# Order of split-precision matmuls within a converted piece of weights: by form instead of by triple

## The chip, the cores and the metric

The kernel runs on one core of a Trainium2 chip. A core has a matrix engine (TensorE, PE in the profile, with its weight loads shown as PEld), VectorE (DVE), ScalarE (ACT), GpSimd (POOL) and SyncE (SP), which issues most DMAs. The metric is the device time of one execution in microseconds; lower is better. Before the change it is 2777.81 us, the median of 3 runs (2772.61 to 2782.02).

## The reference

One decoder residual block over 512 positions with model width 2048, in float32:

```
h = rms_norm(x, norm1_g)
z = h @ w_in                                   # 2048 -> r, k, v, three LoRA inputs, q, k, v, two gates
o_rw  = rwkv7_mix(token_shift(z_rw), ...)      # 16 heads of 64, a recurrence over the positions
o_att = swa_attention(q, k, v, ...)            # 16 query heads, 4 key heads, window 128, sinks
x = x + (sigmoid(z_g1) * (o_rw @ w_b1) + sigmoid(z_g2) * (o_att @ w_b2)) @ w_out
u = rms_norm(x, norm2_g) @ w_up                # 2048 -> 2 x 5632
c = causal convolution of u, width 3
x = x + (silu(c_gate) * c_val) @ w_down        # 5632 -> 2048
```

## The kernel before

Every large matrix product is computed from split operands. A float32 operand `a` becomes a high part `whi` (or `xhi`, `hhi`; type float32r, 32 bits wide, written by ScalarE) and a low part `wlo` (`xlo`, `hlo`; bfloat16, written by VectorE as the difference). `top(x)` reads the upper 16 bits of each element of a high part as bfloat16, so with a stride of two. One product of two 128-deep tiles is then three matmuls that add into the same PSUM bank: high x high (32-bit), top x low (16-bit), low x top (16-bit). They are called a triple here. A 32-bit matmul is one instruction of the program that brings its own weight load; a 16-bit one is a separate LDWEIGHTS and a MATMUL. In the profile both loads are PEld rows.

A "piece" is what one conversion covers, one `whi` and one `wlo` tile. Three places use pieces:

- `project` (L273), the input projection and the two branch projections. A piece is four 128 x 128 weight tiles (`load_w`, 256 KB); the moving operand is 512 positions wide. 352 pieces: 72 output tiles of four pieces, then 32 of two. The matmuls go into the list `stream`. While the input projection runs, attention and the RWKV-7 recurrence run beside it: their small PE steps (L531 to L875) are placed between matmuls of the stream, some of them tied by `behind` to a counted place in `stream`. A scheduler orders the rest of this stage on every engine by its own costs.
- `steps_of` (L1042), the output projection ("o") and the down projection ("dn"). Both are done as seven products of half size (Strassen's way, `PRODUCTS`), added in the two groups of PSUM banks X and Y. A piece is 128 x 1024 weights as the moving operand, in two halves `e` of 512; the stationary operand is two tiles `t` of `hhi`, `hlo`. So a piece has four triples, one for each PSUM bank. There are 210 pieces. At the end of each product `taken_out` (L1064) adds the four banks into the result on VectorE; behind the last product the result is stored.
- `Block.mm` (L1182), the up projection, also in seven products of half size ("P1" to "Q4") for each of 44 column blocks. A piece has eight weight tiles of 128 x 128; the moving operand is 256 positions wide. 308 pieces of eight triples. The order on each engine is the program's (`pin`): `prep(i + 2)` converts the piece after next, `mm(i)` multiplies, `out(i)` takes the PSUM bank away.

Converted tiles lie in rings: four deep for `project` (`wp["hl"]`), three deep for the other two (`hlp`). A `whi` tile is free again when the last matmul that reads it, or its upper halves, is done.

Of the kernel before, what the change touches and what calls it, by code (L numbers as in the profile page):

```python
# [19 lines left out]
P = 128  # L20
S = 512
NT = S // P
# [113 lines left out]
def block_kernel(ctx: ExitStack, tc: tile.TileContext, d: Dims, a: dict, out: bass.AP):  # L136
    nc = tc.nc
    act, dve, pool, pe, sync = nc.scalar, nc.vector, nc.gpsimd, nc.tensor, nc.sync
# [54 lines left out]
    def rsqrt_small(pl, ss, scale, eps, mx=None, tag="rq"):  # L193
        n = ss.shape[-1]
        tl = [pl.tile([P, 8], F32, name=f"{tag}{i}", tag=f"{tag}{i}", bufs=2)[:, :n] for i in range(3)]
        v, y, t = tl
        if mx is not None:
            dve.tensor_scalar(v, ss, mx, None, op0=ALU.max)
        else:
            dve.tensor_scalar(v, ss, scale, eps, op0=ALU.mult, op1=ALU.add)  # L200
        dve.tensor_scalar(t.bitcast(I32), v.bitcast(I32), 1, None, op0=ALU.logical_shift_right)
        dve.tensor_scalar(y.bitcast(I32), t.bitcast(I32), -1, 0x5F3759DF, op0=ALU.mult, op1=ALU.add)
        dve.tensor_scalar(v, v, -0.5, None, op0=ALU.mult)
        for _ in range(3):
            dve.tensor_tensor(t, y, y, op=ALU.mult)
            dve.tensor_tensor(t, t, v, op=ALU.mult)
            dve.scalar_tensor_tensor(y, t, 1.5, y, op0=ALU.add, op1=ALU.mult)
        return y

    pin = tc.keep_in_program_order  # L210
# [9 lines left out]
    def quarter(w, src, c):  # L220
        return sum_d[w][src][c] if isinstance(src, str) else a["w_" + w][src[0], src[1], 2 * c : 2 * c + 2]

    jobs, up_jobs = [], []
    for f in range(NPRE):
        w, t = a["w_up"][f], {n: up_d[f, n] for n in ("s3", "s1", "P6", "P3")}
# [19 lines left out]
    stream = []  # L245

    def top(x):
        x = x.bitcast(BF16)
        return x[(slice(None),) * (len(x.shape) - 1) + (slice(1, None, 2),)]
# [5 lines left out]
    def load_w(src):  # L255
        nk, ncol = src.shape[1:]
        n = nk * ncol
        raw = wp["raw"].tile([P, 512], F32, name="raw", tag="raw")[:, :n].rearrange("p (k c) -> p k c", c=ncol)
        wp["last"] = sync.dma_start(raw, src)
        hi = wp["hl"].tile([P, 512], F32R, name="whi", tag="whi")[:, :n].rearrange("p (k c) -> p k c", c=ncol)  # L260
        lo = wp["hl"].tile([P, 512], BF16, name="wlo", tag="wlo")[:, :n].rearrange("p (k c) -> p k c", c=ncol)
        act.activation(hi, raw, AF.Copy)  # L262
        dve.tensor_tensor(lo, raw, hi.bitcast(F32), op=ALU.subtract)  # L263
        wp["n"] += 1
        if wp["n"] in wp["after"]:
            wp["after"].pop(wp["n"])()
        elif wp["step"] == 3 and wp["n"] <= HELD:
            pass
        elif wp["n"] % wp["step"] == 0 or wp["n"] in extra:
            sums_along()()  # L270
        return hi, lo

    def project(acc, src, xhi, xlo, pre=()):  # L273
        nk = src.shape[1]
        for k0 in range(0, nk, 4):
            n = min(4, nk - k0)
            whi, wlo = pre[k0 // 4] if k0 // 4 < len(pre) else load_w(src[:, k0 : k0 + n])
            for j in range(n):
                k = k0 + j
                first, last = k == 0, k == nk - 1  # L280
                stream.append(pe.matmul(acc, whi[:, j], xhi[:, k], start=first, stop=False))  # L281
                stream.append(pe.matmul(acc, top(whi[:, j]), xlo[:, k], start=False, stop=False))  # L282
                stream.append(pe.matmul(acc, wlo[:, j], top(xhi[:, k]), start=False, stop=last))  # L283


    id16 = cstp.tile([P, P], F16, name="id16")
    def big(pl, nm, tag, dt=F32R):
        return pl.tile([P, BIG], dt, name=nm, tag=tag)

    def by_k(t, n=NK):  # L290
        return t[:, : n * S].rearrange("p (k s) -> p k s", s=S)
# [3 lines left out]
    if True:  # L295
        xhi = by_k(big(big1, "xhi", "h1"))
        xlo = by_k(big(big1, "xlo", "l1", BF16))
# [5 lines left out]
        first = {d.c_ka: []}  # L303
# [29 lines left out]
        def ztile(c0):  # L333
            acc = accp.tile([P, S], F32, name="acc", tag="acc")
            project(acc, zt[c0], xhi, xlo, first.pop(c0, ()))
            return acc
# [5 lines left out]
        r = rsqrt_small(p0, ssum, 1.0 / d.D, RMS_EPS)  # L342
        spread = []
        with tc.tile_pool(name="x0_ps", bufs=1, space=PSUM) as ps0:
            ps = ps0.tile([P, S], F32, name="ps_r")
# [53 lines left out]
        with ExitStack() as pt:  # L399
# [4 lines left out]
            def small():  # L404
                return mps.tile([P, S], F32, name="mi", tag="mi")
# [53 lines left out]
            for t in range(1, NKV):  # L459
                for c0, then in ((d.c_ka, keys), (d.c_va, values)):  # L460
                    acc = ztile(c0 + t * P)
# [25 lines left out]
            for g in range(NHK):  # L487
# [7 lines left out]
                for n in range(NT):  # L495
                    ts = slice(n * P, (n + 1) * P)
                    k0 = 0 if n else BLK
                    nk = 2 * BLK - k0
# [13 lines left out]
                    mx, es, den, rc = (st[:, i] for i in range(4))  # L512
# [15 lines left out]
                    for kb in kbs:  # L528
                        ps = small().rearrange("p (h c) -> p h c", c=P)
# [3 lines left out]
                    ps = small()  # L533
                    for kb in kbs:
                        for i in range(2):
                            pe.matmul(ps, vhl[:, n - 1 + kb, g].rearrange("p e c -> p (e c)"),  # L536
                                      phl[i][:, kb].rearrange("p h c -> p (h c)"),
                                      start=kb == kbs[0] and i == 0, stop=kb == kbs[-1] and i == 1)
                    ol = ap_.tile([HD, S], F32, name="ol", tag="ol", bufs=2)
                    act.activation(ol, ps[HD:P], AF.Copy)  # L540
                    ps, ol = (x[0:HD].rearrange("p (e j c) -> p e j c", e=2, c=P) for x in (ps, ol))
# [5 lines left out]
        with ExitStack() as pr:  # L547
# [18 lines left out]
            def wtile(tag, bufs=1):  # L566
                return wk.tile([P, S], F32, name=tag, tag=tag, bufs=bufs)
# [10 lines left out]
            acc = ztile(d.c_wd)  # L578
# [5 lines left out]
            acc = ztile(d.c_ad)  # L584
# [3 lines left out]
            for i in range(NG):  # L588
                acc = ztile(d.c_gd + i * P)
                t = wtile("lw")  # L590
# [353 lines left out]
    KH = NK // 2  # L944
    TH = S // 2
    NQW = DH // S
# [25 lines left out]
    with ExitStack() as pbb:  # L972
# [8 lines left out]
        for m, i in order:  # L981
            hi, lo, r0, n, gi = parts[i]
# [9 lines left out]
            acc = accp.tile([P, S], F32, name="acc", tag="acc")  # L992
            project(acc, a["w_b"][m].rearrange("p (k c) -> p k c", c=P)[:, r0 : r0 + n], hi, lo)
            if second:
                w = min(XC, d.D)
                for e in range(m * XC, (m + 1) * XC, w):
                    t, c0 = divmod(e, d.D)
# [31 lines left out]
    def raw_tile(nm="raw", n=6):  # L1029
        return rwp.tile([P, WC], F32, name=nm, tag=nm, bufs=n)  # L1030
# [11 lines left out]
    def steps_of(w, i, acc, c, pl, got=None):  # L1042

        _, start, src, _, _ = PRODUCTS[i]
        make, hhi, hlo = got or fetch(w, i, c, pl)
        if not got:
            make()
        for q in range(2):
            wr = raw_tile()
            sync.dma_start(wr, quarter(w, src, c)[q])  # L1050
            whi, wlo = (hlp.tile([P, WC], t, name=f"w{e}", tag=f"w{e}") for e, t in (("hi", F32R), ("lo", BF16)))
            act.activation(whi, wr, AF.Copy)  # L1052
            dve.tensor_tensor(wlo, wr, whi.bitcast(F32), op=ALU.subtract)  # L1053
            fst, lst = start and c + q == 0, c == NB[w] - 1 and q == 1
            for t in range(NT // 2):
                ts = slice(t * P, (t + 1) * P)
                for e in range(NQW):
                    dst, es = acc[t][e], slice(e * S, (e + 1) * S)
                    for j, (l, r) in enumerate((
                            (hhi[:, q, ts], whi[:, es]), (hlo[:, q, ts], top(whi[:, es])), (top(hhi[:, q, ts]), wlo[:, es]))):  # L1060
                        pe.matmul(dst, l, r, start=fst and j == 0, stop=lst and j == 2,  # L1061
                                  skip_group_check=True)

    def taken_out(i, acc, xr, scale, done):  # L1064
        ci, tj, sign = PRODUCTS[i][4]
# [86 lines left out]
    class Block:  # L1152
# [29 lines left out]
        def mm(self, n):  # L1182
            if n == "P1":
                x = ups.tile([P, S], F32, name="X", tag="X")
                self.X = x[:, :TH]
                self.Z = x[:, TH:] if self.f < NPRE else upy.tile([P, S], F32, name="Z", tag="Y")[:, :TH]
            if n == "P7":
                self.Y = upy.tile([P, S], F32, name="Y", tag="Y")[:, :TH]
            into = {"P2": "Z", "P7": "Y", "Q4": "Y"}.get(n, "X")
            ps = getattr(self, "Z" if self.apart and n in ("P5", "P3") else into)  # L1190
            start = n in ("P1", "P7") or n == "P2" and self.f >= NPRE or n == "P5" and self.apart
            whi, wlo = (x.rearrange("p (k c) -> p k c", c=P) for x in self.hl.pop(n))
            xh, xl = bq[{"P1": "b11", "P2": "b21", "P7": "t3", "P6": "t2", "P5": "t1", "Q4": "t4", "P3": "b22"}[n]]
            for k in range(KH):
                last = k == KH - 1
                for i, (l, r) in enumerate(((whi[:, k], xh[:, k]), (top(whi[:, k]), xl[:, k]), (wlo[:, k], top(xh[:, k])))):
                    pin(pe.matmul(ps, l, r, start=start and k + i == 0, stop=last and i == 2,  # L1197
                                  skip_group_check=True))

        def out(self, n):  # L1200
            if n == "P7":
# [140 lines left out]
    with tc.tile_pool(name="sqp", bufs=1, side="right", reuse_waits="tile") as sqp:  # L1342
        yx = ExitStack()
        py = yx.enter_context(tc.tile_pool(name="psY", bufs=1, space=PSUM, side="right", reuse_waits="tile"))
        acc = {"X": banks(px, "X"), "Y": banks(py, "Y")}
        for i in range(len(PRODUCTS)):
            nm = PRODUCTS[i][0]
            last = i == len(PRODUCTS) - 1
# [113 lines left out]
    with ExitStack() as pd:  # L1462
        pxy = pd.enter_context(tc.tile_pool(name="psD", bufs=1, space=PSUM, reuse_waits="tile"))
        acc = {n: banks(pxy, n) for n in "YX"}
# [94 lines left out]
```

## Time and profile before

| | |
|---|---|
| median of 3 runs | 2777.81 us (2772.61 to 2782.02) |
| profiled execution, its time | 2778.65 us |
| its span | 2776.9 us |
| PE busy | 2730.4 us (98%) |
| DVE busy | 2000.0 us (72%) |
| ACT busy | 1341.0 us (48%) |
| DMA moved | 623.80 MB, mean 225 GB/s |
| input projection, attention and RWKV | about 10 to 1130 us of the span |
| branch projections | about 1130 to 1305 us |
| output projection | about 1305 to 1460 us |
| up projection | about 1460 to 2348 us |
| down projection | about 2348 to 2772 us |

The profile is of one execution. A row of the timeline gives start (us from the span's start), duration (us), engine, line, operation, output and inputs with shapes, and how many instructions it stands for; in brackets the idle time of the engine before it and what ended it. A row of weight loads is PEld; the time between the starts of two neighbours says how fast the array takes them, since the duration of one record reaches beyond the start of the next. A row of the waits gives who waited for what: us in total, how often, and the longest. A row of busy time in a stretch gives the stretch, its length, then PE, PEld, DVE, ACT and POOL busy with their counts, the granted clock, the share of the DMA engines and GB/s.

### The profile page before, as it was taken

How to read it: one execution, taken by the hardware profiler on the slowest of the kernel's cores; microseconds unless marked ns; L12 is line 12 of the kernel's file. 1: busy time of each engine (PE TensorE's matmuls, PEld its weight loads, DVE VectorE, ACT ScalarE, POOL GpSimd, SP SyncE). 2: the span in 40 equal slices, each digit the busy share in tenths (PEclk: the TensorE clock that was granted, in tenths of full speed). 3: DMA queues.
4: the chain of work that ended last, by engine and by line, in shares of the span. 5: the costliest groups of instructions: out<-in, count | busy, mean ns of one | idle time of the engine just before them, and what ended most of it. 6: DMA issues, size and time to landing. Idle time of an engine off the chain costs nothing.

```text
span 2776.9 us, 45675 instructions
## 1 busy us (share of the span) xinstructions
PE 2730.4 (98%) x17227; PEld 1705.7 (61%) x17410; DVE 2000.0 (72%) x3476; ACT 1341.0 (48%) x2245; POOL 232.0 (8%) x308
## 2 busy tenths in 40 slices
PE   8999999999999999999999999999999999999999
PEld 3454555555555555444448788888888887444444
DVE  6787777787787774545678788787878788555555
ACT  5455435544544553322465555545554545444443
POOL 0001111111111001011000011111110110000000
PEclk9999999999999999999999999999999999999999
DMA  6557788778878767788775888988898888877775
GB/s 230 151 157 206 202 208 214 207 188 234 219 200 214 178 175 231 241 247 274 246 255 187 235 230 230 246 240 233 225 245 242 226 233 259 303 241 239 253 255 184
DMA packets 228333, 623.80 MB, mean 225 GB/s; under 512 B 24960, under 2 KB 45072, under 8 KB 227088
## 3 DMA queue, kind: packets, MB, share of 16 engines
q1 hardware_dynamic: 159552, 445.23, 49.0%
q0 software_dynamic: 37216, 136.33, 25.4%
q10 hardware_dynamic: 31344, 39.31, 4.1%
q8 instruction: 136, 2.23, 0.3%
q14 instruction: 85, 0.70, 0.1%
HBM read 571.16 MB, written 191.18 MB: 275 GB/s over the span
## 4 chain that ended last, share of the span: by engine, by line
PE 83%; DVE 8%; DMA 3%; issue 3%; ACT 2%; SPq 0%; POOL 0%; ACTq 0%; DVEq 0%; POOLq 0%
PE X L1197 17%; PE X L1061 10%; PE acc L281 9%; PE acc L283 9%; PE Y L1061 9%; PE Y L1197 8%; PE acc L282 8%; PE Z L1197 4%; DVE wlo L263 1%; PE psG L820 1%; PE psS L829 1%; DMA rsb<-rsd 1%; PE bulk L757 1%; PE bulk L805 1%; PE mi L536 1%
## 5 line engine op out<-in xcount | busy, mean ns | idle before, releaser
L281 PE MATMUL acc<-xhi,whi 128*128 128x512 f32 x1152 | 666.4, 578 | 10.5 <-ACT whi L262 10.4
L283 PE MATMUL acc<-xhi,wlo 128*128 128x512 bf16 x1108 | 432.5, 390 | 6.3 <-DVE wlo L263 1.4
L282 PE MATMUL acc<-xlo,whi 128*128 128x512 bf16 x1079 | 423.0, 392 | 0.0
L1053 DVE TENSOR_TENSOR wlo<-raw,whi 128x1024 bf16<-128x1024 f32 x210 | 256.9, 1225 | 203.9 <-ACT whi L1052 202.4
L262 ACT ACTIVATE whi<-raw 128x512 fp32r<-128x512 f32 x352 | 220.3, 627 | 336.4 <-PE acc L282 249.5
L1052 ACT ACTIVATE whi<-raw 128x1024 fp32r<-128x1024 f32 x210 | 221.8, 1057 | 287.6 <-PE X L1061 116.5
L282 PEld LDWEIGHTS <-whi 128*128 128x128 bf16 x1408 | 141.6, 101 | 329.7 <-issue 321.0
L263 DVE TENSOR_TENSOR wlo<-raw,whi 128x512 bf16<-128x512 f32 x352 | 239.7, 688 | 127.9 <-ACT whi L262 116.2
L281 PEld LDWEIGHTS acc<-xhi,whi 128*128 128x128 f32 x1152 | 220.1, 191 | 123.5 <-ACT whi L262 12.8
L1197 PEld LDWEIGHTS <-whi 128*128 128x128 bf16 x2464 | 239.0, 97 | 90.6
L1180 DVE TENSOR_TENSOR wlo<-raw,whi 128x1024 bf16<-128x1024 f32 x184 | 224.9, 1223 | 75.3 <-ACT whi L1178 74.1
L1061 PE MATMUL X<-whi,hhi 128*128 128x512 f32 x480 | 276.9, 577 | 0.1
L1197 PE MATMUL X<-b,whi 128*128 128x256 f32 x1472 | 272.2, 323 | 0.2 <-ACT whi L1178 0.2
L1197 PE MATMUL X<-t,whi 128*128 128x256 f32 (+1 forms) x1408 | 260.3, 323 | 1.5 <-ACT u L1225 1.5
L1197 PE MATMUL Y<-t,whi 128*128 128x256 f32 (+1 forms) x1408 | 260.4, 323 | 0.0
L1197 PEld LDWEIGHTS <-wlo 128*128 128x128 bf16 x2464 | 246.4, 100 | 4.7 <-DVE wlo L1180 4.7
L1178 ACT ACTIVATE whi<-a 128x1024 fp32r<-128x1024 f32 x124 | 130.7, 1054 | 203.5 <-DVE a L1173 199.9
L1061 PEld LDWEIGHTS <-hlo 128*128 128x128 bf16 x840 | 80.6, 96 | 212.2 <-issue 212.2
L1061 PE MATMUL Y<-whi,hhi 128*128 128x512 f32 x360 | 207.8, 577 | 0.0
L1197 PE MATMUL X<-b,wlo 128*128 128x256 bf16 x736 | 204.3, 278 | 1.1 <-DVE wlo L1180 1.1
L1178 ACT ACTIVATE whi<-raw 128x1024 fp32r<-128x1024 f32 x184 | 192.5, 1047 | 20.8 <-ACT whi L1178 13.0
L1180 DVE TENSOR_TENSOR wlo<-a,whi 128x1024 bf16<-128x1024 f32 x124 | 151.9, 1225 | 66.9 <-ACT whi L1178 66.2
(387 smaller groups left out, 5398.0 us busy)
## 6 DMA issues: line engine op xcount, KB each, us to landing
raw<-in_w_up_dram SPq DMA_DIRECT2D x170, 512.0 KB
raw<-in_w_z_dram SPq DMA_DIRECT2D x288, 256.0 KB
s_dn<-in_w_dn_dram POOLq DMA_DIRECT2D x88, 512.0 KB, 7.4
raw<-s_dn SPq DMA_DIRECT2D x88, 512.0 KB
raw<-in_w_up_dram POOLq DMA_DIRECT2D x80, 512.0 KB, 8.5
raw<-in_w_dn_dram SPq DMA_DIRECT2D x66, 512.0 KB
s_dn<-in_w_dn_dram SPq DMA_DIRECT2D x44, 512.0 KB
s_dn<-s_dn SPq DMA_DIRECT2D x44, 512.0 KB
```

The source lines that it names most:

```text
L262: act.activation(hi, raw, AF.Copy)
L263: dve.tensor_tensor(lo, raw, hi.bitcast(F32), op=ALU.subtract)
L281: stream.append(pe.matmul(acc, whi[:, j], xhi[:, k], start=first, stop=False))
L282: stream.append(pe.matmul(acc, top(whi[:, j]), xlo[:, k], start=False, stop=False))
L283: stream.append(pe.matmul(acc, wlo[:, j], top(xhi[:, k]), start=False, stop=last))
L536: pe.matmul(ps, vhl[:, n - 1 + kb, g].rearrange("p e c -> p (e c)"), phl[i][:, kb].rearrange("p h c -> p (h c)"), start=kb == kbs[0] and i ...
L1052: act.activation(whi, wr, AF.Copy)
L1053: dve.tensor_tensor(wlo, wr, whi.bitcast(F32), op=ALU.subtract)
L1061: pe.matmul(dst, l, r, start=fst and j == 0, stop=lst and j == 2, skip_group_check=True)
L1178: pin(act.activation(hi, t, AF.Copy))
L1180: return lambda: pin(dve.tensor_tensor(lo, t, hi.bitcast(F32), op=ALU.subtract))
L1197: pin(pe.matmul(ps, l, r, start=start and k + i == 0, stop=last and i == 2, skip_group_check=True))
```

## The change

In all three places the order of the matmuls of one piece is changed, and nothing else. Before, the triples follow each other. Now all high x high matmuls of the piece come first, then all top x low, then all low x top. The flags that open and close an accumulation move with the first and the last matmul of a bank. The number of matmuls and loads, the operands, the conversions and the transfers are the same.

```diff
 project:
-            for j in range(n):
-                k = k0 + j
-                first, last = k == 0, k == nk - 1
-                stream.append(pe.matmul(acc, whi[:, j], xhi[:, k], start=first, stop=False))
-                stream.append(pe.matmul(acc, top(whi[:, j]), xlo[:, k], start=False, stop=False))
-                stream.append(pe.matmul(acc, wlo[:, j], top(xhi[:, k]), start=False, stop=last))
+            ops = [[(whi[:, j], xhi[:, k0 + j]) for j in range(n)],
+                   [(top(whi[:, j]), xlo[:, k0 + j]) for j in range(n)],
+                   [(wlo[:, j], top(xhi[:, k0 + j])) for j in range(n)]]
+            for i, part in enumerate(ops):
+                for j, (l, r) in enumerate(part):
+                    stream.append(pe.matmul(acc, l, r, start=k0 + i + j == 0, stop=k0 + n == nk and i == 2 and j == n - 1))
 steps_of:
-            for t in range(NT // 2):
-                ts = slice(t * P, (t + 1) * P)
-                for e in range(NQW):
-                    dst, es = acc[t][e], slice(e * S, (e + 1) * S)
-                    for j, (l, r) in enumerate((
-                            (hhi[:, q, ts], whi[:, es]), (hlo[:, q, ts], top(whi[:, es])), (top(hhi[:, q, ts]), wlo[:, es]))):
-                        pe.matmul(dst, l, r, start=fst and j == 0, stop=lst and j == 2,
-                                  skip_group_check=True)
+            for j in range(3):
+                for t in range(NT // 2):
+                    ts = slice(t * P, (t + 1) * P)
+                    for e in range(NQW):
+                        dst, es = acc[t][e], slice(e * S, (e + 1) * S)
+                        l, r = ((hhi[:, q, ts], whi[:, es]), (hlo[:, q, ts], top(whi[:, es])), (top(hhi[:, q, ts]), wlo[:, es]))[j]
+                        pe.matmul(dst, l, r, start=fst and j == 0, stop=lst and j == 2, skip_group_check=True)
 Block.mm:
-            for k in range(KH):
-                last = k == KH - 1
-                for i, (l, r) in enumerate(((whi[:, k], xh[:, k]), (top(whi[:, k]), xl[:, k]), (wlo[:, k], top(xh[:, k])))):
-                    pin(pe.matmul(ps, l, r, start=start and k + i == 0, stop=last and i == 2,
-                                  skip_group_check=True))
+            for i in range(3):
+                for k in range(KH):
+                    l, r = ((whi[:, k], xh[:, k]), (top(whi[:, k]), xl[:, k]), (wlo[:, k], top(xh[:, k])))[i]
+                    pin(pe.matmul(ps, l, r, start=start and k + i == 0, stop=k == KH - 1 and i == 2, skip_group_check=True))
```

Three places on PE, in the order of the built program. A row is line, operation, output<-inputs and the output's size; a MATMUL without an LDWEIGHTS ahead of it is a 32-bit one.

First a product of the up projection (Y is the PSUM bank, t the factor on the right in its two parts). Before:

```order
L1197 MATMUL Y<-t_15027,whi 128x256
L1197 LDWEIGHTS whi
L1197 MATMUL Y<-t_15028,whi 128x256
L1197 LDWEIGHTS wlo
L1197 MATMUL Y<-t_15027,wlo 128x256
```

Now (the pairs of LDWEIGHTS and MATMUL are each there eight times; the start is shown):

```order
L1196 MATMUL Z<-b_13632,wlo 128x256
L1196 MATMUL Y<-t_15027,whi 128x256 x8
L1196 LDWEIGHTS whi
L1196 MATMUL Y<-t_15028,whi 128x256
L1196 LDWEIGHTS whi
```

Eight 32-bit matmuls now stand in a row, and one change from 32 to 16 bits is left where there were eight.

Second a step of the recurrence beside the input projection: psU (L823) and psS (L829) are steps of the RWKV chain, between them lie copies on ScalarE and VectorE; acc is a bank of the projection. Before:

```order
L281 MATMUL acc<-xhi,whi 128x512
L823 MATMUL psU<-GY,BX 128x128
L282 LDWEIGHTS whi
L282 MATMUL acc<-xlo,whi 128x512
L283 LDWEIGHTS wlo
L283 MATMUL acc<-xhi,wlo 128x512
L281 MATMUL acc<-xhi,whi 128x512
L282 LDWEIGHTS whi
L282 MATMUL acc<-xlo,whi 128x512
L283 LDWEIGHTS wlo
L283 MATMUL acc<-xhi,wlo 128x512
L829 MATMUL psS<-UV,W_2861 128x64 x2
```

Now:

```order
L823 MATMUL psU<-GY,BX 128x128
L283 LDWEIGHTS wlo
L283 MATMUL acc<-xhi,wlo 128x512
L283 MATMUL acc<-xhi,whi 128x512 x2
L829 MATMUL psS<-UV,W_2861 128x64 x2
L283 MATMUL acc<-xhi,whi 128x512 x2
```

The steps of the chain still stand between matmuls of the projection and cut some pieces; here three of these stand between psU and psS where there were five. All steps from psU to psS together have 230 where there were 240.

Third the last piece of the down projection (X with four numbers are its four PSUM banks). Before:

```order
L1061 MATMUL X_25473<-whi,hhi 128x512
L1061 LDWEIGHTS hlo
L1061 MATMUL X_25473<-whi,hlo 128x512
L1061 LDWEIGHTS hhi
L1061 MATMUL X_25473<-wlo,hhi 128x512
L1061 MATMUL X_25474<-whi,hhi 128x512
L1061 LDWEIGHTS hlo
L1061 MATMUL X_25474<-whi,hlo 128x512
L1061 LDWEIGHTS hhi
L1061 MATMUL X_25474<-wlo,hhi 128x512
```

Now:

```order
L1061 LDWEIGHTS hhi
L1061 MATMUL X_25471<-wlo,hhi 128x512 [waits DVE_49]
L1061 LDWEIGHTS hhi
L1061 MATMUL X_25472<-wlo,hhi 128x512
L1061 LDWEIGHTS hhi
L1061 MATMUL X_25473<-wlo,hhi 128x512
L1061 LDWEIGHTS hhi
L1061 MATMUL X_25474<-wlo,hhi 128x512
```

The last matmuls of the four banks, which `taken_out` waits for, now follow each other directly at the very end.

## The prediction

> **What bounds the kernel now.** I read the page's totals and its chain first, then PE's waits, then single matmuls in the timeline.
>
> ```profile
> span 2776.9 us, 45675 instructions
> PE 2730.4 (98%) x17227; PEld 1705.7 (61%) x17410; DVE 2000.0 (72%) x3476; ACT 1341.0 (48%) x2245; POOL 232.0 (8%) x308
> PE 83%; DVE 8%; DMA 3%; issue 3%; ACT 2%; SPq 0%; POOL 0%; ACTq 0%; DVEq 0%; POOLq 0%
> PE X L1197 17%; PE X L1061 10%; PE acc L281 9%; PE acc L283 9%; PE Y L1061 9%; PE Y L1197 8%; PE acc L282 8%; PE Z L1197 4%; DVE wlo L263 1%; PE psG L820 1%; PE psS L829 1%; DMA rsb<-rsd 1%; PE bulk L757 1%; PE bulk L805 1%; PE mi L536 1%
> ```
>
> TensorE sets the time: 83% of the chain that ended last, and nearly all of that on the three places that the diff touches (L281 to L283, L1061, L1197). A busy PE is not PE at its peak, because a matmul's record is longer than the step to the next. So I work with steps between starts. First the up projection (L1197, 256 columns); the first row is from the chain of waits, the next four are weight loads, the last two matmuls.
>
> ```profile
> 2308.56 2.83 PE X L1197 x24
> ...
> 2000.18 0.19 PEld L1197 LDWEIGHTS Z<-b,whi 128*128 128x128 f32 x1
> 2000.41 0.10 PEld L1197 LDWEIGHTS <-whi 128*128 128x128 bf16 x1
> 2000.42 0.10 PEld L1197 LDWEIGHTS <-wlo 128*128 128x128 bf16 x1
> 2000.53 0.19 PEld L1197 LDWEIGHTS Z<-b,whi 128*128 128x128 f32 x1
> ...
> 2000.18 0.28 PE L1197 MATMUL X<-t,wlo 128*128 128x256 bf16 x1
> 2000.53 0.28 PE L1197 MATMUL Z<-b,wlo 128*128 128x256 bf16 x1
> ```
>
> 24 matmuls take 2.83 us: 0.3538 a triple. The 32-bit load starts with the wlo matmul before it (2000.18), so it is fetched ahead, under that matmul. The 16-bit load of whi starts only 0.23 later, when wlo and the 32-bit matmul are both through: 0.115 each. It is not fetched ahead of a 32-bit matmul. From there to the next wlo matmul are 0.12 (2000.41 to 2000.53), in which lie the load of whi and its matmul. The second 16-bit load follows 0.01 to 0.02 behind the first: that much a 16-bit load holds up what comes behind it. The same at 512 columns, L1061 and L281:
>
> ```profile
> 1400.39 0.19 PEld L1061 LDWEIGHTS X<-whi,hhi 128*128 128x128 f32 x1
> 1400.83 0.10 PEld L1061 LDWEIGHTS <-hlo 128*128 128x128 bf16 x1 [0.25 <-issue]
> 1401.08 0.19 PEld L1061 LDWEIGHTS X<-whi,hhi 128*128 128x128 f32 x1
> ...
> 1007.07 0.19 PEld L281 LDWEIGHTS acc<-xhi,whi 128*128 128x128 f32 x1
> 1007.53 0.10 PEld L282 LDWEIGHTS <-whi 128*128 128x128 bf16 x1 [0.27 <-issue]
> 1007.54 0.10 PEld L283 LDWEIGHTS <-wlo 128*128 128x128 bf16 x1
> 1007.76 0.19 PEld L281 LDWEIGHTS acc<-xhi,whi 128*128 128x128 f32 x1
> ```
>
> Triples of 0.69, split 0.44 and 0.25 (L1061), 0.46 and 0.23 (L281). Each triple has one change from a 32-bit to a 16-bit matmul, and at each the 16-bit load stands open.
>
> **The change, part by part.** No matmul, load, conversion or transfer is added or taken away. What goes are changes of form: in the built order 2464 become 308 in the up products, 839 become 210 at L1061, 1257 become 331 in the projections (pieces are split by other PE work there). 3711 go.
>
> What takes their place are 32-bit matmuls behind 32-bit ones, and 16-bit ones behind 16-bit ones with their loads fetched ahead. The trace has the first at 512 columns, six in a row at L875; and loads of both forms in rows of eight with 128 columns (L740 32-bit, L805 16-bit).
>
> ```profile
> 410.50 0.40 PE L875 MATMUL bulk<-gdlo,wghi 128*128 128x512 f32 x1
> ...
> 411.66 0.40 PE L281 MATMUL acc<-xhi,whi 128*128 128x512 f32 x1
> 410.51 0.19 PEld L875 LDWEIGHTS bulk<-gdhi,wglo 128*128 128x128 f32 x1
> 410.74 0.19 PEld L875 LDWEIGHTS bulk<-gdhi,wghi 128*128 128x128 f32 x1
> 1000.24 1.04 PE L740 MATMUL bulk<-ident,BKK 128*128 128x128 f32 x8
> 1000.13 0.90 PEld L740 LDWEIGHTS bulk<-ident,BKK 128*128 128x128 f32 x8
> 335.14 0.62 PE L805 MATMUL bulk<-id,XIW 128*128 128x128 f16 x8 [0.38 <-DVE XIW L801]
> ...
> L740 PE MATMUL bulk<-ident,BKK x64: 272/272/273, 323.4 to 1001.0; 128*128 128x128 f32 x64
> L805 PE MATMUL bulk<-id,XIW x256: 217/219/230, 335.1 to 1035.0; 128*128 128x128 f16 x128
> ```
>
> Five steps from 410.50 to 411.66 are 0.232 each, and each load starts with the matmul before it: 32-bit behind 32-bit is fetched ahead. Its step is what 32-bit costs in a triple (0.44 to 0.46 for two), within 0.005. At 256 columns no row shows it. The nearest are L740's loads: eight in 0.90, less one record of 0.19, over seven: 0.101 each; and their matmuls, less one record of 0.272 (the median in ns in the last rows), (1.04 - 0.272) / 7 = 0.11. Half of L875's step is 0.116, today's triple gives 0.115, so a 32-bit load just fits under a matmul of 256. I take 0.115, with 0.13 as the poor end (a load plus 0.02 of handing over). 16-bit behind 16-bit: L805, (0.62 - 0.219) / 7 = 0.057 for 128 columns, so at most 0.115 for 256 and 0.23 for 512.
>
> So a change of form that goes is worth, at the least, 0.3538 - 3 x 0.115 = 0.009 at 256 columns and 0.69 - 3 x 0.23 = 0 at 512. At the most it is worth L1061's 0.25 less 0.23, 0.02, or 0.025 with the rounding of the rows. I take 0.015, the 0.01 to 0.02 of the load that stands open, since it is the part that the order of loads shows directly.
> - Up products: 2156 x 0.015 = 32 us.
> - L1061: 629 x 0.015 = 9 us.
> - Projections: 926 x 0.015 = 14 us, of which I leave 5 out, for the reason of the next rows.
> - 32-bit behind 32-bit at 512, 0.232 against 0.23: 1629 x 0.002 = 3 us lost.
>
> A section of the Trainium skill bears on this: TensorE: Matmul & The Clock Gate, Back-to-back issue gap, gives columns / 2.4 GHz + 2.5 ns for a warm matmul, 215.7 ns at 512 columns and 109.2 at 256, whatever the form. L875's 0.232 disagrees for 32-bit operands. By it alone, used as an estimate, the sum would be some 160 us instead of 55.
>
> The waits around the change, all from the waits view (whole RWKV stretch, then up stage):
>
> ```profile
> PEld psS L829 <- DVE UV L825: 15.7, 47, 0.4
> PEld L805 <- DVE XIW L801: 9.4, 30, 0.9
> PEld L1197 <- DVE wlo L1180: 4.7, 8, 0.9
> ```
>
> In the RWKV pairs PE already waits for VectorE at 47 of the chunk steps. Between psU (L823) and psS (L829) stand three to seven projection matmuls; if these go faster there, PE waits the difference. In the built order a few of these steps also lose a matmul or two of cover (240 become 230 in all, 10 x 0.23 = 2.3 us). Hence the 5 us. In the up stage PE waited 4.7 us for wlo, at most 0.9 at once. Now 16 matmuls (16 x 0.115 = 1.8 us) stand ahead of the first use of wlo, so I count 4 us won. The whi buffers come free earlier, at two thirds of a piece, wlo at the same place as before; ACT's conversions can only start earlier.
>
> The end of the program loses. The last product's four outputs were finished a triple apart, and are now finished one matmul apart:
>
> ```profile
> 2770.38 2.75 DVE L1073 TENSOR_TENSOR xa<-xa,X 128x512 f32<-128x512 f32 x4 [4.08 <-PE X L1061]
> 2772.03 0.38 PE L1061 MATMUL X<-wlo,hhi 128*128 128x512 bf16 x1
> ```
>
> PE ended at 2772.41, the adds at 2773.13. Now the first add can start 3 x 0.23 = 0.69 before PE's end and the four still take 2.75: they end 2.06 behind PE, where they ended 0.72. That costs 1.3 us. At the other products' ends the adds lie beside the next product's matmuls.
>
> What is late next? VectorE and the DMAs carry the same work in less time:
>
> ```profile
> 1460.00:2340.00 880.00, 874.38 (x7399) 752.61 (x7399) 704.81 (x853) 467.11 (x637) 88.01 (x102) 1.00 0.85 232
> 2360.00:2365.00 5.00, 4.92 (x22) 2.23 (x23) 1.30 (x2) 2.39 (x3) 0.00 (x0) 1.00 1.03 424
> ```
>
> In the up stage VectorE is busy 705 of 880 us, and would be of about 845: 83%. The DMAs move 232 GB/s there, though they are busy 0.85; at 2360 they moved 424. Neither binds at 4% more. The granted clock is 1.00 throughout.
>
> Sum: 32 + 9 + 14 - 5 - 3 + 4 - 1.3 = 50 us. From the profiled execution's 2778.65 (0.84 above the median of the runs) that gives 2729.
>
> **The rivals.**
> - The gap is not the load. The step of 0.12 from whi to wlo is what a 16-bit matmul of 256 columns takes in any order, and the open load costs nothing. For it: 0.23 at L281 is no longer than L875's step. Then only the waits and the end move: 2773 to 2779, no change. Against it: whi's step counts from its own load's start, and L805 gives 0.115 or less for 256.
> - 32-bit loads do not fit under 256 columns. A load's record is 0.19; if it held the array that long, 32-bit behind 32-bit would step 0.19 instead of 0.115, and the up products would lose 2156 x 0.075 = 162 us: 2729 + 162 = 2891, slower. It decides from a step of about 0.138 on, where 2156 x 0.023 eats the 50. Against it: L740's steps of 0.10 to 0.11 with the same load, and the 32-bit load under a wlo matmul of 256 in today's triple, which leaves 0.115 for both.
> - Much more. All forms step by the lower bound of today's rows, 0.12 - 0.015 = 0.105 at 256 and 0.23 - 0.015 = 0.215 at 512: triples of 0.315 and 0.645, 2464 x 0.039 + 2248 x 0.045 = 197 us, less the 849 changes that remain, at about 0.045 each (38 us): about 160 us, 2619. Against it stands L875. The skill's section above is the rule that gives this time.
> - The gain is eaten elsewhere: the RWKV chains keep all 14 us and VectorE's order of conversions, which the scheduler redraws in that stage, costs 15 more: 2729 + 9 + 15 = 2753.
>
> **How the numbers follow.** My case 0.62; gain half eaten 0.13; no change 0.10; slower by loads 0.10; much more 0.05. A change under 0.3% (8 us) can't be told from none. Faster: 0.62 + 0.13 + 0.05 = 0.80; same 0.10; slower 0.10. The likeliest case has 2691 (3711 x 0.025 = 93 us, less the same 5 us of small terms) to 2765 (2156 x 0.009 = 19 us, less them) as its own range. To hold 8 in 10 the range must take in the case of no change: 2695 to 2779, without the slower case, the much faster one, and the corner of 0.025.
>
> **What would show it.** In the profile after: at L1196 a product of 24 matmuls in about 2.72 us instead of 2.83, with 32-bit loads 0.115 apart; idle PEld ahead of the first 16-bit load alone; at L1061 groups of four 32-bit matmuls 0.23 apart; longer PEld waits at L829; the adds at the end of the program starting 0.7 before PE's end. It is wrong if 32-bit loads in a row stand 0.13 or more apart at 256 columns, or if 16-bit matmuls in a row still step 0.12.

## The result and the profile after

The changed kernel takes 2743.15 us (median of 4 runs, 2739.42 to 2744.4) against 2778.95 for the kernel before, beside which it ran: a ratio of 0.9872, 95% interval 0.9852 to 0.9892. Timed again later, beside other kernels, it had 2739.58 against 2773.96: 0.9881, 0.9864 to 0.9897. So it is 1.2 to 1.3% faster, about 35 us. The forecast was 2729 with a range of 2695 to 2779.

The profiled execution has 2743.16 us. The totals and the chain of its page:

```profile
span 2741.3 us, 45720 instructions
PE 2685.9 (98%) x17227; PEld 1832.6 (67%) x17410; DVE 1995.1 (73%) x3476; ACT 1334.9 (49%) x2245; POOL 231.3 (8%) x308
PE 83%; DVE 8%; DMA 4%; ACT 2%; issue 2%; SPq 0%; DVEq 0%; ACTq 0%
PE acc L283 27%; PE X L1196 16%; PE X L1061 11%; PE Y L1061 9%; PE Y L1196 8%; PE Z L1196 4%; DMA raw<-in_w_z_dram 1%; DVE wlo L263 1%; PE psS L829 1%; PE psG L820 1%; PE bulk L757 1%; DMA rsb<-rsd 1%; PE bulk L805 1%; DVE wlo L1179 1%; PE psU L823 1%
```

TensorE is still 83% of the chain; the work is the same and PE is the bound as before. The next rows are one product of the up projection, now at L1196, first as the chain of waits merges it, then its weight loads in the timeline:

```profile
2308.10 2.75 PE Z L1196 x24
```

```profile
2000.00 1.01 PEld L1196 LDWEIGHTS X<-t,whi 128*128 128x128 f32 x8
2001.06 0.77 PEld L1196 LDWEIGHTS <-whi 128*128 128x128 bf16 x8
2001.85 0.89 PEld L1196 LDWEIGHTS <-wlo 128*128 128x128 bf16 x8
2002.75 0.19 PEld L1196 LDWEIGHTS X<-b,whi 128*128 128x128 f32 x1
```

A product takes 2.75 us instead of 2.83. The three groups can be read from the starts of their loads. The 32-bit loads begin under the last matmul of the product before, and 1.06 later comes the first 16-bit load: less that one matmul (0.114) this is 0.118 for each of the eight 32-bit matmuls. The whi group has 0.79 to the next group, the wlo group 0.90, which is 0.113 each. Between single whi matmuls the median step in the trace is 0.109, and the first has 0.122, since its load stands open. So whi gained (0.124 with its open load before, 0.109 now), wlo about stayed, and the 32-bit matmuls lost a little (0.115 before, if the 0.227 of one wlo and one 32-bit matmul is split evenly).

The same at 512 columns, a piece of the output projection:

```profile
1400.61 0.87 PEld L1061 LDWEIGHTS X<-whi,hhi 128*128 128x128 f32 x4
1401.76 0.57 PEld L1061 LDWEIGHTS <-hlo 128*128 128x128 bf16 x4 [0.27 <-issue]
1402.45 0.54 PEld L1061 LDWEIGHTS <-hhi 128*128 128x128 bf16 x3
```

One idle stretch ahead of a 16-bit load is left for four triples. Median steps are 0.236 between 32-bit matmuls, 0.227 for hlo (its moving operand is the upper halves, two apart) and 0.215 for the contiguous wlo.

By stages (from the first matmul of one to the first of the next, before and after):

| stage | before | after | difference |
|---|---|---|---|
| input projection, attention, RWKV | 1118.4 | 1116.5 | -1.9 |
| branch projections | 177.5 | 173.4 | -4.1 |
| output projection | 158.2 | 156.4 | -1.8 |
| up projection | 886.1 | 862.3 | -23.8 |
| down projection, to the start of PE's last matmul | 424.0 | 418.8 | -5.2 |

The first row is within chance: in six profiles with the old order there (the kernel before, and experiments below) the stage has 1112 to 1118 us, in six with the new order 1109 to 1120. Part of the chance is the granted clock: before the change it was 0.83 in two stretches of 10 us of this stage (from 30 and from 380), after it in one (from 570), and 0.17 x 10 is up to 1.7 us each.

The end of the program and the waits of the RWKV pairs, from the timeline and from the waits view:

```profile
2734.51 1.02 PE L1061 MATMUL X<-wlo,hhi 128*128 128x512 bf16 x4
2734.93 2.48 DVE L1072 TENSOR_TENSOR xa<-xa,X 128x512 f32<-128x512 f32 x4 [6.03 <-PE X L1061]
```

```profile
PEld psS L829 <- DVE UV L825: 19.1, 48, 0.5
PEld L805 <- DVE XIW L801: 17.4, 32, 1.1
PEld psU L823 <- DVE GY L821: 10.0, 38, 0.3
PEld L757 <- DVE XIW L217: 9.3, 20, 0.8
```

PE ends at 2735.53, the four adds at 2737.41, 1.88 behind it; before the change they ended 0.72 behind it. And PE waits longer for the RWKV chain: L805 17.4 us instead of 9.4, L829 19.1 instead of 15.7.

### The profile page after: what moved, and what is told of

Its sections match the earlier page's. It is cut to its first block, busy times and chain, and to the rows that moved or that the text cites. A ratio compares the mean times of both kernels' runs of the same rounds, so it can differ in the third digit from the quotient of the medians.

```text
span 2741.3 us, 45720 instructions
## 1 busy us (share of the span) xinstructions
PE 2685.9 (98%) x17227; PEld 1832.6 (67%) x17410; DVE 1995.1 (73%) x3476; ACT 1334.9 (49%) x2245; POOL 231.3 (8%) x308
## 4 chain that ended last, share of the span: by engine, by line
PE 83%; DVE 8%; DMA 4%; ACT 2%; issue 2%; SPq 0%; DVEq 0%; ACTq 0%
PE acc L283 27%; PE X L1196 16%; PE X L1061 11%; PE Y L1061 9%; PE Y L1196 8%; PE Z L1196 4%; DMA raw<-in_w_z_dram 1%; DVE wlo L263 1%; PE psS L829 1%; PE psG L820 1%; PE bulk L757 1%; DMA rsb<-rsd 1%; PE bulk L805 1%; DVE wlo L1179 1%; PE psU L823 1%
## 5 line engine op out<-in xcount | busy, mean ns | idle before, releaser
L283 PE MATMUL acc<-xhi,whi 128*128 128x512 f32 x1152 | 377.9, 441 | 10.7 <-ACT whi L262 10.3
L283 PE MATMUL acc<-xhi,wlo 128*128 128x512 bf16 x1107 | 311.8, 388 | 2.6
L283 PE MATMUL acc<-xlo,whi 128*128 128x512 bf16 x1080 | 302.1, 384 | 4.0 <-issue 0.5
L1196 PEld LDWEIGHTS <-wlo 128*128 128x128 bf16 x2464 | 237.4, 96 | 39.5
L1196 PEld LDWEIGHTS <-whi 128*128 128x128 bf16 x2464 | 216.9, 98 | 34.7
L1177 ACT ACTIVATE whi<-a 128x1024 fp32r<-128x1024 f32 x124 | 130.8, 1055 | 223.0 <-DVE a L1172 208.5
L283 PEld LDWEIGHTS <-wlo 128*128 128x128 bf16 x1408 | 134.5, 98 | 155.6 <-issue 5.3
L1177 ACT ACTIVATE whi<-raw 128x1024 fp32r<-128x1024 f32 x184 | 192.1, 1045 | 3.3 <-PE X L1196 1.6
L1196 PE MATMUL X<-b,whi 128*128 128x256 f32 (+1 forms) x1472 | 192.1, 283 | 0.7 <-ACT whi L1177 0.3
L1196 PE MATMUL X<-t,whi 128*128 128x256 f32 (+1 forms) x1408 | 183.8, 283 | 2.9 <-ACT u L1223 2.5
L1196 PE MATMUL Y<-t,whi 128*128 128x256 f32 (+1 forms) x1408 | 183.8, 283 | 0.4 <-DVE u L1225 0.4
L1061 PE MATMUL X<-whi,hhi 128*128 128x512 f32 x480 | 153.3, 441 | 1.4 <-ACT whi L1052 1.4
L1061 PEld LDWEIGHTS <-hhi 128*128 128x128 bf16 x840 | 81.5, 97 | 103.7
L1247 DVE SCALAR_TENSOR_TENSOR c<-u,par,c 128x512 f32<-128x512 f32 x176 | 131.5, 747 | 14.2 <-ACT c L1244 14.0
```

Source lines behind the costliest of these rows:

```text
L283: stream.append(pe.matmul(acc, l, r, start=k0 + i + j == 0, stop=k0 + n == nk and i == 2 and j == n - 1))
L1177: pin(act.activation(hi, t, AF.Copy))
L1196: pin(pe.matmul(ps, l, r, start=start and k + i == 0, stop=k == KH - 1 and i == 2, skip_group_check=True))
L1247: pin(dve.scalar_tensor_tensor(t, u[:, i, j + 1 : j + 1 + S], cw[:, j + 1, ci : ci + 1], t, op0=ALU.mult, op1=ALU.add))
```

## The experiments

Theory A: what is won is the open 16-bit load at each change from 32 to 16 bits, less what 32-bit matmuls in a row cost more. Theory B: in the RWKV pairs PE's gain becomes waiting for the chain. The rivals stand with each.

**Each place alone.** Three kernels, each the kernel before with one of the three places in the new order.

```diff
 e1: Block.mm     for k: for i in range(3):   ->   for i in range(3): for k:
 e2: project      for j: three matmuls        ->   three groups over j
 e3: steps_of     for t: for e: for j         ->   for j: for t: for e
```

> The new order in the up projection alone; the other two places as before. Theory A (each 32-to-16-bit change that goes saves the open 16-bit load, less what 32-bit behind 32-bit costs more): 308 products x 0.080 us (2.827 to 2.747 in the two traces), so 24 to 25 us faster than before, and the up stage about 862 us long. Rival W (the gain comes from waits: wlo is needed later and whi is free earlier): a product's undisturbed 24 matmuls stay at 2.83 us and at most the 15 us of disturbed products move.

> The new order in the input and branch projections alone. Theory B (in the RWKV pairs PE waits for the chain, so only the stretches without the chain gain): branch stage 4 us shorter, the start of the input projection 5 us shorter, the pairs the same or a little longer: 4 to 8 us in all. Rival P (the projections gain everywhere, and what the pairs lost is lost to the other changes): 352 pieces x 0.064 us = 22 us.

> The new order in the output and down projection alone. Theory A: 210 pieces, 5 to 8 us faster, with the adds at the end of the program about 2.1 us behind PE's last matmul instead of 0.7. With the two kernels above it adds up to the whole change's 36 us, if the three places don't touch each other.

Measured, as ratios to the kernel before: up alone 0.9901 (0.9886 to 0.9916), 27 us; projections alone 0.9976 (0.9967 to 0.9986), 7 us; output and down projection alone 0.9976 (0.9966 to 0.9985), 7 us. Together 41 us, the whole change 33 to 36: they add up within their intervals, each about 3 to 4 us wide to either side. In e3 the adds at the end come 1.87 us behind PE's last matmul, where 2.1 were expected. In e1's trace the up stage has 861.9 us, as with the whole change, and its products 2.75:

```profile
2204.61 2.75 PE X L1197 x24
2207.36 2.75 PE Y L1197 x24
```

So 24 to 27 of some 35 us are the up projection, and the products themselves became shorter: rival W, that waits alone did it, falls. For e2 the branch stage is 173.4 as with the change, the input stage 1117.9 against 1118.4: nothing is won there. Rival P's 22 us are excluded.

The 5 us that theory B gave to the start of the input projection were half won and lost again. The next rows are the attention steps beside it (L536) and the first step of the RWKV pairs (L706), with what PE waited for ahead of that step; first e1, which has the old order there, then e2:

```profile
L536 PE MATMUL mi<-phi,vhl x28: 387/494/505, 123.0 to 247.3; 128*128 128x512 f32 x28
L706 PE MATMUL bulk<-BAR,BKK x16: 379/379/483, 311.4 to 316.5; 128*128 128x256 f32 x16
  DVE BAR L688: 1.5, 1
```

```profile
L536 PE MATMUL mi<-phi,vhl x28: 387/481/506, 120.6 to 246.1; 128*128 128x512 f32 x28
L706 PE MATMUL bulk<-BAR,BKK x16: 379/379/483, 311.0 to 316.0; 128*128 128x256 f32 x16
  DVE BAR L688: 3.3, 1
```

At the first attention step e2 is 2.4 us ahead, at the last 1.2, at the first step of the pairs 0.4 (the changed kernel has 1.2 there), and its wait for VectorE ahead of that step is 1.8 us longer. So the gain of the start, too, goes into waits.

**How many changes of form.** The up projection alone, by form within groups of two or four weight tiles, and once with 32-bit and top x low matmuls in turn.

```diff
-            for k in range(KH):
-                for i in range(3):
+            for k0 in range(0, KH, 2):          # e9: 4
+                for i in range(3):
+                    for k in range(k0, k0 + 2): # e9: 4
 e10:
+            (whi, xh), (top whi, xl) for each k, then (wlo, top xh) for each k
```

> The up projection alone, by form within every two weight tiles instead of eight: four changes from 32 to 16 bits a product, where there were eight and the change has one. Theory A (a price for each change): four of the seven go, 4/7 of 24.5 = 14 us faster than before, products of 2.78 us. Rival W (the later use of wlo and the earlier release of whi): wlo is needed as the fifth matmul, so at most 3 us faster. Rival G (only long groups gain, because the first matmul of each group pays for it): less than 7 us.

> The up projection alone, by form within every four weight tiles: two changes from 32 to 16 bits a product. Theory A in the form that the runs so far give it (0.015 us won for each change that goes, 0.004 lost for each 32-bit matmul that stands in a group): 6 x 0.015 - 8 x 0.004 = 0.058, a product of 2.77 us between 2.80 for twos and 2.747 for eights. Rival G (the gain goes with the number of changes alone, 0.080 / 7 for each): 6/7 of it, 2.758.

> The up projection alone: a product takes 32-bit and top x low matmuls in turn for its eight tiles, then all eight low x top. As many changes from 32 to 16 bits as before (eight), no two 32-bit ones in a row, wlo needed only after 16 matmuls and whi free as early as with the change. Theory A: no change goes, so a product of 2.82 to 2.83 us as before. Rival W (the later use of wlo and the earlier release of whi, or 16-bit matmuls in a row as such): 2.75 to 2.78.

Products in the chain of waits, of e4, e9 and e10:

```profile
2204.47 2.80 PE Z L1198 x24
```

```profile
2207.47 2.76 PE X L1198 x24
```

```profile
2203.31 2.87 PE Z L1197 x24
```

Twos: 2.80 us (median 2.800), and 0.9963 of the time before (0.9951 to 0.9976), 10 us faster where 14 were expected; that is over the 3 us of rival W, and not clearly over the 7 of e4's rival G. The other two have one time each: fours 2752.88 and both forms in turn 2785.68, beside 2775.06 before. Fours: 2.756. Eights: 2.747. So the gain rises with the changes that go, 0.027, 0.071 and 0.080 for four, six and seven of them, but not evenly: 0.007, 0.012 and 0.011 each. Fours met rival G's 2.758 and not the 2.77 of theory A with fixed prices; twos met neither (theory A 2.78, G by its even price 2.78). Part of the unevenness can be read from the starts of the load groups: one 32-bit and one wlo matmul together take 0.227 us in triples, 0.2325 in pairs, 0.231 in fours and 0.232 in eights (with 0.109 for a whi matmul). So what 32-bit matmuls in a row lose is lost with pairs already, while the open loads go on falling away. Why it is a little more in pairs than in fours was not tried and stays open.

The kernel with both forms in turn decides against W. It needs wlo late, frees whi early, and has eight 16-bit matmuls in a row, yet its products take 2.87, more than before the change. That is also 0.05 more than theory A said. Its loads show where:

```profile
2000.24 0.10 PEld L1197 LDWEIGHTS <-whi 128*128 128x128 bf16 x1
2000.24 0.20 PEld L1197 LDWEIGHTS X<-t,whi 128*128 128x128 f32 x1
2000.49 0.10 PEld L1197 LDWEIGHTS <-whi 128*128 128x128 bf16 x1
```

A 16-bit and a 32-bit matmul in turn take 0.246 a pair (2000.24 to 2000.49), where the triple before has 0.115 + 0.124 = 0.239 for the two. Eight times 0.007 are 0.056. So the count of changes explains it where W doesn't; that the other 0.007 is the price of a 32-bit load right behind an open 16-bit one is a reading of these rows and was not tried by itself.

**The RWKV pairs.** Three kernels ask why the pairs won nothing; the changed kernel itself ran beside the first two.

> The changed kernel itself, timed again beside the next three so that they can be compared with it: 2740 to 2746 us, ratio to before 0.987.

It had 2739.58 us and 0.9881 (above), just below what was expected. First the triples kept while the pairs run, and the tied places of the chain moved:

```diff
 e5, in project:  + if wp.get("triples"): the three matmuls of each j in turn   # set from the first pair to the last
 e6:
-            LATER = (24, 30, ZT, ZT + 30, 2 * ZT + 8, 2 * ZT + 34, 3 * ZT + 12, 5 * ZT + 42)
+            LATER = (24, 30, ZT + 1, ZT + 32, 2 * ZT + 11, 2 * ZT + 38, 3 * ZT + 17, 5 * ZT + 42)
               # FIRST and LAST alike; the last place of FIRST from 5 * ZT + 40 to + 42
```

> The changed kernel, but the input projection keeps the triples while the RWKV pairs run (the stretch before them and the branch projections keep the new order). Theory B (a pair is bound by its chain, PE's gain becomes waiting): the same time as the changed kernel within 3 us, an undisturbed pair 95.8 us as in both kernels so far, the PE waits at L805, L757, L823 and L829 back to those of before (35 us in all, against 57). Rival R (the new order does harm in the pairs, by splitting groups and by a worse order on VectorE): 4 to 6 us faster than the changed kernel.

> The changed kernel with the entries of the five inverse levels of each RWKV pair tied one projection matmul later each, counted up (5 matmuls more ahead of the last level and behind it the same order). Theory B: the chain waits there anyway, so five more matmuls lie under it and five fewer remain after it: 8 pairs x 5 x 0.22 = up to 9 us faster than the changed kernel, undisturbed pairs about 94.7 us, waits at L805 and L757 down by half. Rival R (PE is the bound in the pairs and waits are chance): no change, or up to 5 us slower since the chain is put off.

Both have the time of the changed kernel: 0.9881 (0.9867 to 0.9896) and 0.9886 (0.9871 to 0.9900) beside its 0.9881. With the triples the waits are back where they were (its lines are six further on; L835 is the old L829, L811 L805, L829 L823, L763 L757):

```profile
PEld psS L835 <- DVE UV L831: 16.8, 49, 0.5
PEld L811 <- DVE XIW L807: 8.9, 26, 0.9
PEld psU L829 <- DVE GY L827: 7.2, 32, 0.3
PEld L763 <- DVE XIW L217: 2.6, 8, 0.7
```

These four are 35.5 us, those of the changed kernel 55.8. The new order spares PE some 12 us in the pairs (192 pieces x 0.064), and these four waits are 20 us longer with it, at the same total. Rival R, that the order does harm, would have made e5 4 to 6 us faster; the times alone, with 4 us to either side, don't exclude that, but the pairs do. One pair, read between the transposes at its end (L861), in the kernel before and in the changed one:

```profile
891.96 0.66 PE L861 MATMUL bulk<-ident,yc 128*128 128x128 f32 x4 [0.17 <-DVE yc L854]
987.72 0.66 PE L861 MATMUL bulk<-ident,yc 128*128 128x128 f32 x4
```

```profile
890.71 0.66 PE L861 MATMUL bulk<-ident,yc 128*128 128x128 f32 x4
986.45 0.66 PE L861 MATMUL bulk<-ident,yc 128*128 128x128 f32 x4
```

95.76 and 95.74 us; in e5 the same pair has 95.80. The moved places of e6 changed nothing either. An undisturbed pair has 95.9 us, where 94.7 were expected; its waits at L805 and L757 are 14.2 and 8.9 us in the later pairs' stretch, against 14.1 and 8.7 in the changed kernel that ran beside it. The steps from psU to psS lost as many projection matmuls as the levels won, 47, so it put the cover elsewhere but did not add any; as a test of theory B it tells little.

The next takes much more from PE in the pairs:

```diff
 e8, in project, while the pairs run:
+                    if i == 2 and j == 0: leave this matmul out (its place in stream is kept)
```

> The changed kernel with one matmul left out of each projection piece while the RWKV pairs run (the first low x top of the piece, so those projections are incomplete). 24 pieces of a pair x 0.226 us = 5.4 us less for PE in each pair, 3.6 times what the change itself takes away there (24 x 0.064 = 1.5). Theory B (a pair is bound by its chain): an undisturbed pair falls by less than 2 us, to 94 or more, and PE's waits on the chain (L805, L757, L823, L829, L820) grow by some 25 us or more over the stretch. Rival R (PE is the bound and only chance ate the change's gain): pairs of 90.4 us, 38 us faster in all.

It has 0.9814 (0.9797 to 0.9832), 16 to 19 us faster than the changed kernel with its 0.9872 and 0.9881: less than rival R's 38, more than theory B allowed. Read from one pair's transposes to the next, the first four stretches have 94.9 to 99.4 us, the fifth 91.9 and the sixth 91.2. The fifth:

```profile
797.66 0.66 PE L864 MATMUL bulk<-ident,yc 128*128 128x128 f32 x4 [0.45 <-DVE yc L857]
889.60 0.66 PE L864 MATMUL bulk<-ident,yc 128*128 128x128 f32 x4 [0.46 <-DVE yc L857]
```

```profile
ACT whi L262 <- DMA raw<-in_w_z_dram: 16.0, 11, 2.3
```

In the first four ScalarE waits 16 us for weights (second fence, 400 to 790 us), where the changed kernel has 4.5 in one profile and none in the other; that the loads bind there is likely, but was not tried. Behind them 3.9 and 4.5 of the 5.4 us come through. PE's waits on the five lines of the chain are 82 us against 64 and 67 in the two profiles of the changed kernel (260 to 1060 us): 15 to 18 more, where theory B asked for 25. So the chain is no fixed length that binds by itself, as theory B had it. Shown is that the change's 1.5 us a pair are not seen in the pairs and that the waits grow by at least as much; that the chain's latencies are the only cause is not shown.

**The data of the third group.** The wlo matmuls of the up projection with a contiguous moving operand.

```diff
-            (wlo[:, k], top(xh[:, k]))
+            (wlo[:, k], xl[:, k])
```

> The changed kernel, but the third group of an up product (wlo) reads the low half of the right factor, which is contiguous 16-bit data, in place of the upper halves of its high part, which lie two apart: so the cross term is computed with another operand. In the trace of the changed kernel these matmuls step 0.1135 us, those of the second group, with contiguous data, 0.109. Theory C (data two apart streams slower): 308 x 8 x 0.0045 = 11 us faster than the changed kernel, products 2.71 us. Rival: the step belongs to the place in the product or to the weights (wlo contiguous, whi two apart); then no change.

Its products take 2.71 us, and the wlo loads are 0.109 apart instead of 0.1135 (from 2001.04, the first of eight, to the next product's 32-bit load at 2001.91); one fence each from the chain, the timeline and the waits:

```profile
2228.95 2.71 PE X L1196 x24
```

```profile
2001.04 0.86 PEld L1196 LDWEIGHTS <-wlo 128*128 128x128 bf16 x8
2001.91 1.01 PEld L1196 LDWEIGHTS Y<-t,whi 128*128 128x128 f32 x8
```

```profile
PEld X L1196 <- ACT u L1223: 8.4, 15, 2.8
```

Theory C is right on the step: data two apart streams 4% slower than contiguous 16-bit data at 256 columns. But of 308 x 0.034 = 10.5 us the up stage keeps 3 (859.1 against 862.2), and the time 0.9866 (0.9851 to 0.9880) can't be told from the changed kernel's. The last row has most of the reason: PE waits 8.4 us for ScalarE to take a bank away, where the changed kernel has 3.3. The next thing to bind in the up stage is close.

**The end of the program.** The very last piece keeps its triples.

```diff
+            if w == "dn" and i == len(PRODUCTS) - 1 and c == NB[w] - 1 and q == 1:
+                ops.sort(key=lambda x: x[1:])    # back to t, e, then form
```

> The changed kernel with the triples kept in the very last piece of the down projection. The four adds at the end end 0.7 us behind PE's last matmul, as before the change, and not 1.9 as in the changed kernel: 1.1 us, too little for the times, so it is read from the profile.

```profile
2736.69 2.75 DVE L1073 TENSOR_TENSOR xa<-xa,X 128x512 f32<-128x512 f32 x4 [4.65 <-PE X L1062]
2738.33 0.38 PE L1062 MATMUL X<-wlo,hhi 128*128 128x512 bf16 x1
```

PE ends at 2738.71, the adds at 2739.44: 0.73 behind it, as expected, 1.15 us better than the changed kernel. Its one time, 2744.92, is half a microsecond above the highest of that kernel (2744.4), so the gain can't be told from the times. No version tried is faster than the changed kernel by more than can be told, apart from e8, which leaves work out.

## Why the prediction was right, and where it was off

The mechanism was right: the cause is the 16-bit load that stood open behind each 32-bit matmul, and the likeliest case is the one that came. That the time lies in the range says little by itself, since the range reached up to no change at all; what bears the mechanism out is the products of e1, e4, e9 and e10. The size was 50 us and is 35. By the terms of the sum:

| term | forecast | measured |
|---|---|---|
| up products, changes that go | 32 | 24.6 (308 x 0.080) |
| up stage, waits for wlo | 4 | -0.9 |
| output and down projection, changes that go | 9 | 7.0 with the 32-bit loss in it |
| projections, less what the chain takes | 14 - 5 = 9 | 4.1 in the branches, 1.9 (within chance) in the input stage |
| 32-bit in a row at 512 columns | -3 | in the two rows above |
| end of the program | -1.3 | -1.2 |

Three steps were off, all on one side.
- The price of 32-bit behind 32-bit at 256 columns. I took 0.115 between a lower row and a poor end of 0.13; it is 0.118. 308 x 8 x 0.003 = 7 us, which is nearly the whole of the first row's gap. The open load itself came out as sized: whi went from 0.124 to 0.109, 0.015. These figures rest on the even split of 0.227; with today's 0.1135 for wlo before as well, the load is 0.018 and the loss 0.0045. Either way it is the 32-bit matmuls that fell short. One of the rows that set the lower end was misread: single starts of L740's loads are 0.109 apart, not 0.101, so there was less room under 256 columns than it seemed.
- The waits for wlo. They did go: no row of them is left in the up stage. But the PE stands at the same places now for ScalarE. Products more than 0.06 us above the median cost 15.3 us together before and 16.2 after (15.3 to 15.4 in three profiles with triples there, 15.8 to 17.0 in seven with the new order). The waits in the up stage of the changed kernel:

  ```profile
  PEld X L1196 <- ACT u L1223: 3.3, 3, 2.8
  PEld Z L1196 <- ACT whi L1177: 1.6, 1, 1.6
  PEld X L1196 <- ACT whi L1177: 1.3, 2, 0.7
  ```

  Before, the first had 1.8 us and the other two 1.3 together. I had asked what is late next for the engines' busy time, and not for each of these waits, where ScalarE's conversion of whi and its copies out of PSUM come right behind.
- The input projection. I left 5 of 14 us out for the chain; nearly all of the input projection's share went. Per piece the branches show what was there to win: 4.1 us over 64 pieces, 0.064 each, so 18 us over the 288 pieces of the input projection, and 0 to 2 came. Twelve of the 18 belong to the 192 pieces beside the pairs (e5, and the pairs of 95.76 and 95.74 us); the rest is the start and the end of the stage, where e2 was 2.4 us ahead and had 0.4 left at the first pair. The prediction counted no wait there.

The prediction also read the granted clock as 1.00 throughout; it was 0.83 in two stretches of 10 us of the input stage, and that kind of chance is as large as the 1.9 us of the input stage.

The rivals: that the gap is not the load fell with the whi step of 0.109. That 32-bit loads don't fit under 256 columns fell with 0.118, though the lost 0.003 goes that way. Much more fell with the 32-bit steps of 0.118 and 0.236. The section Back-to-back issue gap of the Trainium skill's page TensorE: Matmul & The Clock Gate (109.2 ns and 215.7 ns by it) gives its formula for an isolated matmul and names no type of operand; here it holds for the contiguous 16-bit groups (0.109 and 0.215 to 0.216) and for no other: two apart 0.1135 and 0.227, 32-bit 0.118 and 0.236. That the gain is eaten elsewhere held for the input projection, but the further 15 us that the redrawn order of conversions was to cost did not come. The end of the program came as worked out.

## What to carry to other kernels

Where 32-bit and 16-bit matmuls mix, count the changes from the first to the second: behind a 32-bit matmul the 16-bit load is not fetched ahead, which cost 0.015 us each time here, and ordering by form within what is converted anyway takes most of them away. The cost here was small: 32-bit matmuls in a row took 0.118 instead of about 0.115, and the end of the program 1.2 us. A step that shortens PE brings only what the next wait leaves, so look for each wait that goes at what stands next behind the same instruction. Where small dependent steps were threaded through the stream, next to nothing came.

## What the runs showed of the hardware

- The step of a matmul goes with its moving operand: contiguous 16-bit 0.109 us at 256 columns, 16-bit two apart 0.1135; 32-bit matmuls in a row, which also bring their own weight loads, 0.118. In e7 the same weights went from 0.1135 to 0.109 with another moving operand alone.
- 32-bit and 16-bit matmuls in turn were the slowest order tried, 0.246 a pair against 0.118 + 0.109 = 0.227 in groups.
